# First swiglu of a two-layer encoder: modulation in four blocks of 256 channels, weight chunks begun two k at a time, six low parts on GpSimd

## Chip, cores and metric

The kernel runs on one core of one Trainium2 chip. The metric is the device time of one execution in microseconds (us); runs are compared by their median. Names of engines: PE is TensorE's matmul side, PEld its weight loads, DVE is VectorE, ACT is ScalarE, POOL is GpSimd, SP is SyncE, whose queue issues all DMAs of this kernel.

## What is computed

A two-layer encoder over 256 tokens of 1024 channels, all in float32. Each layer is swiglu, token mixer, swiglu; each of these sublayers is wrapped alike, with shift, scale and gate computed from a vector c by a 1024 x 9216 matrix per layer:

```python
sc = jax.nn.silu(c)
mod = (sc @ ada_w[i] + ada_b[i]).reshape(B, 9, D)

def modulated_sublayer(x, mod, g_pre, g_post, fn, weight):
    shift, scale, gate = mod[:, 0], mod[:, 1], mod[:, 2]
    h = rmsnorm(x, g_pre) * (1.0 + scale) + shift
    y = rmsnorm(fn(h), g_post)
    return x + weight * (1.0 + gate) * y

def swiglu(h, w_in, w_out):          # w_in 1024 x 5632, w_out 2816 x 1024
    gate, up = jnp.split(h @ w_in, 2, axis=-1)
    return (jax.nn.silu(gate) * up) @ w_out
```

So nothing of the first swiglu can be multiplied before the first 2048 columns of `ada_w[0]` (8 MB: shift and scale) have been loaded, summed and applied.

## The kernel before

The 256 tokens are two tiles t = 0, 1 of 128. A swiglu (class `FFN`) runs over 11 chunks c of 256 hidden channels. For a chunk and a token tile, `inn` multiplies h by 8 k-tiles of 128 channels (512 output columns: 256 gate, 256 up), `act` applies silu and the product, `tr` transposes, and `outt` multiplies by the output weights `wo` into an accumulator. `unit(c, t)` is one such step, with `tr` and `outt` of earlier steps after it.

**Two-part operands.** Most weights are multiplied as two float32r parts: ACT makes the high part (a cast, L263), DVE the low part (a subtraction, L271: raw minus high), and PE makes three passes per k (`mm3`, L98 to L100). Weights "in whole" are multiplied in float32 as loaded, with no work on ACT or DVE; PE then shows two records per k (L794).

**Bulk.** All weight loads are a queue of tasks (class `Bulk`): load, ACT work, DVE work. Loads go through four raw buffers of 1 MB (`N_RAW`), which are used in turn; a load into a buffer waits until the buffer's last reader is done, and SP issues in order, so what stands behind it waits too. Modulation vectors other than the first two come in four pieces of 1 MB (`ada_vector`), summed on DVE in two steps of 1024 columns each (L352: sum += weight row x sc[k]). `plan` spreads such pieces between the weights of a swiglu.

**The first swiglu.** Shift (m = 0) and scale (m = 1) come in halves of 512 channels, each of two 1 MB pieces (`ada_half`); a half takes 8 DVE steps of 512 columns per vector. PE sums over partitions (`finish_cols`, L361) and transposes the scaled x (L562); DVE or ACT modulates (L582, L576). `head_first` runs chunks 0 to 2 while the second half of the channels is on its way: chunks 0 and 2 multiply the first four k in float32, chunk 1 in two parts; `rest` does the other four k of all three, and then come `tr` and `outt` of chunks 0 and 1. Chunk 3 and later ones are `unit` steps. Four pieces of the next sublayer's modulation (`ss1[0]` to `ss1[3]`) stand between the weights of this stretch; the other 18 pieces of f0's plan are spread over chunks 3 to 9.

Of the kernel before, what the change touches and what calls it, by code (L numbers as in the profile page):

```python
# [39 lines left out]
def kernel(  # L40
# [127 lines left out]
    class Bulk:  # L168
        """A queue of loads, each followed by its work on ACT (high parts) and on DVE (low parts, sums).
        Loads run N_RAW entries ahead of the DVE work."""  # L170

# [36 lines left out]
        def high(self, key):  # L208
            """Emit the ACT work up to and including key (whose load must be out)."""
# [47 lines left out]
    def split_work(name, st, put, width=2048):  # L257
        """The two parts of a raw tile (st[0]); put() gets their tiles."""
# [8 lines left out]
        def low(lo_=0, hi_=width, engine=nc.vector):  # L267
# [48 lines left out]
    def ada_half(layer, m, hf, accs, pieces=(1, 1)):  # L316
        """Half of the channels of mod[layer, m], in two 1 MB pieces."""
        st = {}
        wv = ada_w[layer].rearrange("(p k) n -> p k n", k=KD)
        c0 = m * D + hf * 512  # L320

        def load(q):
            def go():
                raw = raw_tile(f"adah{m}{hf}{q}")
                rv = raw.rearrange("p (k n) -> p k n", k=4)
                for k in range(0, 4, 4 // pieces[q]):
                    ks = slice(k, k + 4 // pieces[q])
                    nc.sync.dma_start(rv[:, ks, :], wv[:, 4 * q + ks.start : 4 * q + ks.stop, c0 : c0 + 512])
                st[q] = raw

            return go

        def compute(q):
            def go():
                rv = st.pop(q).rearrange("p (k n) -> p k n", k=4)
                if m not in accs:
                    accs[m] = rowp.tile([P, D], F32, tag="acc", name=f"aacc{layer}{m}", bufs=3)
                acc = accs[m][:, hf * 512 : (hf + 1) * 512]
                for j in range(4):
                    ada_step(acc, rv[:, j, :], 4 * q + j)  # L340
                if q == 1:
                    bulk.fin.append(lambda: finish_cols(layer, m, range(hf * 4, hf * 4 + 4))(acc))

            return go

        return [(("adah", m, hf, q), load(q), None, compute(q)) for q in range(2)]
# [1328 lines left out]
```

## Time and profile before

| | |
|---|---|
| time, median of 3 runs (lowest to highest) | 929.82 us (928.57 to 932.09) |
| profiled execution, first to last instruction (span) | 928.2 us |
| PE busy | 902.1 us, 97% of the span |
| DVE, ACT, POOL busy | 705.8, 441.1, 41.9 us |
| moved by DMA | 235.28 MB, 253 GB/s over the span |
| mean granted TensorE clock | 0.992 of full |

The profiled execution's own time is given by its span alone; what lies around a span is seen in the 1.6 us between it and the median of the runs. An engine's busy time says little of what bounds the kernel where stages differ, so the rows are read by stage: the head (to 78 us, when chunk 3 begins), the body of the first swiglu (78 to 220 us), and the rest. "DMA share" is the mean busy share of the 16 DMA engines (it can read a little over 1), "PEclk" the granted clock as a share of 2.4 GHz. A releaser in brackets is what ended an engine's idle time.

### The profile page before, as it was taken

The numbers are of one execution on the slowest core, as the hardware profiler recorded it, in microseconds if no ns is written. First come the engines' busy times: TensorE is split into PE (matmuls) and PEld (weight loads), VectorE is DVE, ScalarE is ACT, GpSimd is POOL, SyncE is SP. The second block draws the span as 40 slices with busy tenths as digits, with TensorE's granted clock in tenths as the row PEclk, the third lists the DMA queues.
The fourth block names the chain that finished last, engine by engine and source line by source line (L and its number), as shares of the span: only waits on it lengthen the run. The fifth ranks groups of instructions, "written<-read, shape, count | busy, mean of one in ns | idle before, by whom it ended". The sixth has DMA issues, their size and how long they took to land.

```text
span 928.2 us, 11193 instructions
## 1 busy us (share of the span) xinstructions
PE 902.1 (97%) x4251; PEld 741.1 (80%) x4251; DVE 705.8 (76%) x856; ACT 441.1 (48%) x661; POOL 41.9 (5%) x56
## 2 busy tenths in 40 slices
PE   4999999999999999999999999999899999999997
PEld 3578887887888888888888888888798888888885
DVE  5898888788867998897867987766898765656553
ACT  2345443345645434334643534337699654343421
POOL 0000000000000000000000000001163000000000
PEclk9999999999999999999999999998999999999999
DMA  9989998996358998897469899960133558857601
GB/s 324 370 313 352 364 372 311 345 373 210 137 181 287 376 342 323 303 365 268 137 203 371 320 350 322 346 234 32 53 130 100 173 156 278 292 194 259 226 1 45
DMA packets 135973, 235.28 MB, mean 253 GB/s; under 512 B 5628, under 2 KB 98415, under 8 KB 135664
## 3 DMA queue, kind: packets, MB, share of 16 engines
q1 hardware_dynamic: 135920, 234.58, 72.6%
q8 instruction: 33, 0.54, 0.2%
q14 instruction: 20, 0.16, 0.0%
HBM read 233.51 MB, written 1.05 MB: 253 GB/s over the span
## 4 chain that ended last, share of the span: by engine, by line
PE 89%; DVE 4%; ACT 3%; issue 2%; DMA 1%; POOL 0%; SPq 0%; DVEq 0%; POOLq 0%; ACTq 0%
PE acc L747 25%; PE in L100 16%; PE in L98 16%; PE in L99 16%; PE accm L1314 2%; PE ps_g L724 2%; PE ps_h L562 1%; PE ps_mod L361 1%; DVE aacc L352 1%; PE in L794 1%; PE accp L965 1%; DMA adah<-in_ada_w_dram 1%; ACT p L1228 1%; DMA wi<-in_ffn_w_in_dram 1%; PE ps_turn L391 1%
## 5 line engine op out<-in xcount | busy, mean ns | idle before, releaser
L352 DVE SCALAR_TENSOR_TENSOR aacc<-ada,sc,aacc 128x1024 f32<-128x1024 f32 (+1 forms) x113 | 143.8, 1273 | 11.3 <-DMA ada<-in_ada_w_dram 9.1
L708 ACT ACTIVATE sil<-in 128x256 f32<-128x256 f32 x84 | 32.2, 383 | 247.7 <-PE in L100 240.4
L710 DVE TENSOR_TENSOR g<-in,sil 128x256 f32<-128x256 f32 x84 | 35.2, 420 | 52.4 <-ACT sil L708 52.3
L95 DVE TENSOR_TENSOR gL<-ps_g,gH 128x256 fp32r<-128x256 f32 x88 | 36.7, 417 | 23.6 <-ACT gH L94 23.5
L94 ACT CAST gH<-ps_g 128x256 fp32r<-128x256 f32 x88 | 32.4, 368 | 45.1 <-PE ps_g L724 45.0
L503 POOL TENSOR_TENSOR r<-ms,mhalf 128x1 f32<-128x1 f32 x24 | 13.6, 565 | 838.4 <-DVE ms L501 838.4
L724 PEld LDWEIGHTS ps_g<-ident,g 128*128 128x128 f32 x176 | 24.7, 140 | 11.5
L724 PE MATMUL ps_g<-ident,g 128*128 128x128 f32 x176 | 33.6, 272 | 0.0
L508 ACT ACTIVATE junk<-x 128x512 bf16<-128x512 f32 x24 | 15.1, 631 | 21.4 <-DVE x L535 11.3
L361 PE MATMUL ps_mod<-ones,aacc 128*128 128x1 f32 x96 | 12.7, 259 | 10.1 <-DVE cols L150 9.9
L576 ACT ACTIVATE hs<-ps_h,mod,mod 128x128 f32<-128x128 f32 x48 | 18.1, 458 | 8.4 <-DVE mod L377 5.0
L361 PEld LDWEIGHTS ps_mod<-ones,aacc 128*128 128x128 f32 x96 | 13.0, 210 | 11.2 <-DVE cols L150 10.1
L352 DVE SCALAR_TENSOR_TENSOR aacc<-adah,sc,aacc 128x512 f32<-128x512 f32 x28 | 21.0, 752 | 0.9
L582 DVE TENSOR_SCALAR hs<-ps_h,mod,mod 128x128 f32<-128x128 f32 x48 | 16.4, 404 | 5.2 <-PE ps_h L562 4.9
L535 DVE SCALAR_TENSOR_TENSOR x<-tmp,r,x 128x512 f32<-128x512 f32 x23 | 16.3, 749 | 2.2 <-POOL r L503 1.2
L1238 POOL TENSOR_SCALAR p<-p,rs 128x256 f32<-128x256 f32 x16 | 16.1, 1008 | 28.6 <-ACT p L1228 15.3
L554 ACT ACTIVATE xr<-x,r 128x512 f32<-128x512 f32 x12 | 8.7, 722 | 17.4 <-POOL r L503 17.4
L1228 ACT ACTIVATE p<-s,nm 128x256 f32<-128x256 f32 x32 | 14.9, 471 | 3.1 <-DVE nm L1220 2.6
L593 DVE TENSOR_TENSOR hTL<-hs,hTH 128x512 fp32r<-128x512 f32 x24 | 15.6, 688 | 0.4
L562 PE MATMUL ps_h<-ident,xr 128*128 128x128 f32 x96 | 14.3, 292 | 0.5 <-ACT xr L554 0.3
L271 DVE TENSOR_TENSOR wo10L<-wo,wo10H 128x2048 fp32r<-128x2048 f32 x4 | 9.2, 2293 | 7.4 <-ACT wo10H L263 7.4
L1263 PE MATMUL att<-pT,v 128*128 128x256 f32 x52 | 13.8, 389 | 0.5 <-ACT pT L1255 0.3
(498 smaller groups left out, 2892.7 us busy)
## 6 DMA issues: line engine op xcount, KB each, us to landing
wi<-in_ffn_w_in_dram SPq DMA_DIRECT2D x176, 512.0 KB, 5.9
ada<-in_ada_w_dram SPq DMA_DIRECT2D x64, 1024.0 KB, 6.4
wo<-in_ffn_w_out_dram SPq DMA_DIRECT2D x44, 1024.0 KB, 6.2
adah<-in_ada_w_dram SPq DMA_DIRECT2D x6, 1024.0 KB, 10.3
mwo<-in_mla_w_o_dram SPq DMA_DIRECT2D x4, 1024.0 KB, 5.4
bc<-in_ada_b_dram SPq DMA_DIRECT2D x12, 256.0 KB, 6.7
bc<-in_norm_g_dram SPq DMA_DIRECT2D x12, 256.0 KB, 7.4
adah<-in_ada_w_dram SPq DMA_DIRECT2D x4, 512.0 KB, 11.9
```

The lines of the kernel that those rows point to most:

```text
L94: nc.scalar.copy(h, src)
L95: nc.vector.tensor_sub(lo, src, h.bitcast(F32))
L98: nc.tensor.matmul(ps, lhsT=lh, rhs=rh, start=first, stop=False)
L99: nc.tensor.matmul(ps, lhsT=lh, rhs=rl, start=False, stop=False)
L100: nc.tensor.matmul(ps, lhsT=ll, rhs=rh, start=False, stop=last)
L352: nc.vector.scalar_tensor_tensor(acc, w, sc[:, k : k + 1], acc, op0=ALU.mult, op1=ALU.add)
L361: nc.tensor.matmul(ps[:, j : j + 1], lhsT=acc[:, (j - j0) * P : (j - j0 + 1) * P], rhs=ones[:, 0:1], start=True, stop=True,)
L708: nc.scalar.activation(sil, ps[:, 0:CW], AF.Silu)
L710: nc.vector.tensor_mul(g, ps[:, CW : 2 * CW], sil)
L724: nc.tensor.transpose(ps[:, a * P : (a + 1) * P], g[:, a * P : (a + 1) * P], ident)
L747: nc.tensor.matmul(acc[hf], lhsT=lhs[:, a, :], rhs=rhs[:, a, hf * 512 : (hf + 1) * 512], start=f, stop=l)
L1228: nc.scalar.activation(p[:, t * S : (t + 1) * S], ps[:, t * S : (t + 1) * S], AF.Exp, bias=nm[:, t : t + 1], accum_out=sm[:, t : t + 1],)
```

## The change

- Shift and scale of the first swiglu come in four blocks of 256 channels, one raw tile of 1 MB per vector and block (`ada_block`), in two DMAs (four for the first scale block). A block takes 8 DVE steps of 256 columns per vector.
- `head_first` is written anew. Per block b of 256 channels (2 k-tiles): sums, reduction, modulation, then those two k of chunks 0, 1 and 2 for both token tiles. Chunk 0 is multiplied in float32 for all k, chunk 1 for the first four k, chunk 2 always in two parts. Weights of these chunks are loaded two k at a time (`load_whole`, `load_raw`), chunk 2's first two blocks into one raw tile `wrc2`, later blocks of chunks 1 and 2 into `wrb2` and `wrb3`.
- DVE makes the low parts of these weights, but for chunk 2's in blocks 2 and 3, which POOL makes. The output weights' low parts of chunks 3 to 8 are made by POOL too (`low_out`).
- The modulation pieces `ss1[0]` to `ss1[3]` move from the head to f0's plan: 22 pieces instead of 18 over chunks 3 to 9. `Bulk.limit` holds the queue back until the head's own loads are out.
- Small ones: the loads of `norm_g` and `ada_b` rows are issued behind the first block and x0; the columns made of them are copied by ACT instead of DVE; in the head `pre_scale` lets DVE scale the half that is needed first; 5 and 4 warming matmuls instead of 6 and 4.

The core of the diff:

```diff
+    def ada_block(m, b, acc, pieces):
+        st = []
+        wv = ada_w[0].rearrange("(p k) n -> p k n", k=KD)
+        c0 = m * D + b * BW
+        def load():
+            rv = raw_tile(f"adab{m}{b}").rearrange("p (k n) -> p k n", k=KD)
+            n = KD // pieces
+            for k in range(0, KD, n):
+                nc.sync.dma_start(rv[:, k : k + n, :], wv[:, k : k + n, c0 : c0 + BW])
+            st.append(rv)
+        def steps(ks=range(KD)):
+            for k in ks:
+                ada_step(acc[:, b * BW : (b + 1) * BW], st[0][:, k, :], k)
+        return load, steps
...
+            def loads(b):
+                if b < 2:
+                    load_whole(0, b)
+                    load_whole(1, b)
+                    load_raw(2, b, "c2", b)
+                else:
+                    load_whole(0, b)
+                    load_raw(1, b, f"b{b}", 0)
+                    load_raw(2, b, f"b{b}", 1)
+            def split_block(b, low2=nc.vector):
+                for t in range(NT):
+                    split_h(t, b)
+                for c in (1, 2):
+                    if (c, b) in parts:
+                        part_high(c, b)
+                        part_low(c, b, nc.vector if c == 1 else low2)
+            def sum_up(b, mid=nop):
+                bank = tr_tile(f"ps_modb{b}")
+                ada[0, b][1]()
+                mid()
+                reduce(0, b, bank)
+                ada[1, b][1]()
+                reduce(1, b, bank)
+                add()
...
+            sum_up(1)
+            for t in range(NT):
+                modulate(t, 1, True)
+                multiply(0, t, 1)
+            split_block(1)
+            ada[1, 2][0]()
+            loads(2)
+            ada[0, 3][0]()
+            turn_next(2)
+            for c in (1, 2):
+                for t in range(NT):
+                    multiply(c, t, 1)
+            sum_up(2, lambda: ada[1, 3][0]())
+            for t in range(NT):
+                modulate(t, 2, True)
+                multiply(0, t, 2)
+            loads(3)
+            split_block(2, nc.gpsimd)
+            more_bulk(1)
...
-        def low(lo_=0, hi_=width, engine=nc.vector):
+        def low(lo_=0, hi_=width, engine=low_engine or nc.vector):
...
-    f0, f2, f3, f5 = FFN(0, 0), FFN(0, 1), FFN(1, 0), FFN(1, 1)
+    f0 = FFN(0, 0, {c: nc.gpsimd for c in range(3, 9)})
+    f2, f3, f5 = FFN(0, 1), FFN(1, 0), FFN(1, 1)
...
-    f0.plan(ss1[4:] + gate(0, 0, in_parts=False) + ss2[:4] + gate(0, 1, hold="pool") + ss2[4:6], first_chunk=4, extra_out=2)
+    f0.plan(ss1 + gate(0, 0, in_parts=False) + ss2[:4] + gate(0, 1, hold="pool") + ss2[4:6], first_chunk=4, extra_out=2)
```

**DVE in the head.** In these rows `aacc00` and `aacc01` are the sums of shift and scale, `mod` their columns, `hs` the modulated h, `hTL` its low part. Before, from the first half's modulation to the sums of the second half:

```order
L582 TENSOR_SCALAR hs00_212<-ps_h00_176,mod01_209,mod00_139 128x128 x4
L350 TENSOR_SCALAR aacc00_111<-adah010_119,sc_93 128x512
L352 SCALAR_TENSOR_TENSOR aacc00_111<-adah010_119,sc_93,aacc00_111 128x512 x3
L593 TENSOR_TENSOR hTL0_173<-hs00_212,hTH0_172 128x512
L588 CAST hTH1_174<-hs10_217 128x512
L593 TENSOR_TENSOR hTL1_175<-hs10_217,hTH1_174 128x512
L271 TENSOR_TENSOR wi10L_245<-wi10_125,wi10H_243 128x2048
L352 SCALAR_TENSOR_TENSOR aacc00_111<-adah011_157,sc_93,aacc00_111 128x512 x4
```

Changed, from block 0's modulation to block 1's columns; what follows for blocks 2 and 3 has the same form:

```order
L834 TENSOR_SCALAR hs00_202<-ps_h0_171,mod01_198,mod00_156 128x128 x2
L492 SCALAR_TENSOR_TENSOR ms_208<-s2_178 128x1
L547 TENSOR_SCALAR xr1_212<-x1_81,r_210 128x512
L95 TENSOR_TENSOR hTL0_99<-hs00_202,hTH0_98 128x256
L95 TENSOR_TENSOR hTL1_101<-hs10_217,hTH1_100 128x256
L798 TENSOR_TENSOR wi20L_234<-wrc2_122,wi20H_233 128x1024
L341 TENSOR_SCALAR aacc00_96<-adab01_125,sc_93 128x256
L343 SCALAR_TENSOR_TENSOR aacc00_96<-adab01_125,sc_93,aacc00_96 128x256 x7
L341 TENSOR_SCALAR aacc01_97<-adab11_157,sc_93 128x256
L343 SCALAR_TENSOR_TENSOR aacc01_97<-adab11_157,sc_93,aacc01_97 128x256 x7
L365 TENSOR_TENSOR mod00_156<-ps_modb1_256,cols_95 128x2
L365 TENSOR_TENSOR mod01_198<-ps_modb1_256,cols_95 128x2
```

The sums of the next channels stood ahead of `hTL` and the weight's low part; now they stand behind them.

**SP's queue in the head**, changed, with the semaphores that each DMA waits for (`DVE` is a wait for the last DVE reader of the raw buffer):

```order
L619 DMA wrc2_122<-in_ffn_w_in_dram 128x2x256 [waits DMAHW2_49]
L330 DMA adab02_193<-in_ada_w_dram 128x4x256 [waits DMAHW3_49,DVE_49]
L330 DMA adab02_193<-in_ada_w_dram 128x4x256 [waits DMAHW4_49]
L330 DMA adab12_294<-in_ada_w_dram 128x4x256 [waits DMAHW5_49,DVE_49]
L330 DMA adab12_294<-in_ada_w_dram 128x4x256 [waits DMAHW6_49]
L619 DMA wi01_297<-in_ffn_w_in_dram 128x2x256 [waits DMAHW7_49]
```

The raw tiles are taken in the order adab00, adab10, wrc2, adab01, adab11, adab02, adab12, so that `adab12` goes into `wrc2`'s buffer, whose last reader is the DVE subtraction of block 1 (the second `wi20L`, behind block 1's sums).

**POOL**, changed; the eight subtractions in the middle are new there:

```order
L494 TENSOR_TENSOR r<-ms,mhalf 128x1 x2
L798 TENSOR_TENSOR wi21L<-wrb_300,wi21H 128x1024
L798 TENSOR_TENSOR wi21L<-wrb_368,wi21H 128x1024
L273 TENSOR_TENSOR wo3L<-wo_658,wo3H 128x2048
L273 TENSOR_TENSOR wo4L<-wo_787,wo4H 128x2048
L273 TENSOR_TENSOR wo5L<-wo_926,wo5H 128x2048
L273 TENSOR_TENSOR wo6L<-wo_1070,wo6H 128x2048
L273 TENSOR_TENSOR wo7L<-wo_1213,wo7H 128x2048
L273 TENSOR_TENSOR wo8L<-wo_1347,wo8H 128x2048
L494 TENSOR_TENSOR r<-ms,mhalf 128x1 x16
```

Before, POOL held only the small powers (`r`) up to the attention; these subtractions were on DVE.

## Rows read from the trace of the kernel before

**Rows 1.** The page: busy time of each engine.
```profile
PE 902.1 (97%) x4251; PEld 741.1 (80%) x4251; DVE 705.8 (76%) x856; ACT 441.1 (48%) x661; POOL 41.9 (5%) x56
```

**Rows 2.** Busy time by stage: PE, PEld, DVE, ACT, POOL, PEclk, DMA share, GB/s.
```profile
24.20:78.01 53.81, 53.11 (x211) 37.19 (x211) 47.97 (x59) 24.07 (x30) 0.00 (x0) 0.97 0.98 343
78.01:220.00 141.99, 141.99 (x649) 116.22 (x648) 118.98 (x116) 58.10 (x66) 1.10 (x2) 1.00 0.99 352
...
48.00:52.00 4.00, 3.96 (x17) 2.77 (x16) 3.96 (x3) 1.96 (x2) 0.00 (x0) 1.00 0.22 59
```

**Rows 3.** Waits of PE from 60 to 300 us: total, times, longest.
```profile
PE in L98 <- DVE hTH L588: 0.5, 1, 0.5
```

**Rows 4.** Timeline of the head: start, us, instruction, idle before and releaser.
```profile
2.11 0.94 SPq L328 DMA_DIRECT2D adah<-in_ada_w_dram  x2
...
7.60 0.48 DVE L350 TENSOR_SCALAR aacc<-adah,sc 128x512 f32<-128x512 f32 x1 [6.22 <-DMA adah<-in_ada_w_dram]
...
11.51 0.63 ACT L508 ACTIVATE junk<-x 128x512 bf16<-128x512 f32 x1 [8.91 <-DMA x<-in_x_dram]
...
27.00 1.90 ACT L263 CAST wi10H<-wi 128x2048 fp32r<-128x2048 f32 x1 [1.19 <-DMA wi<-in_ffn_w_in_dram]
```

**Rows 5.** The chain that ended last, 22 to 43 us: start, us, what.
```profile
22.25 1.07 PE ps_mod L361 x8
...
23.74 0.42 DVE hs L582
...
24.20 8.83 PE in L794 x16
...
33.26 0.23 PE first L99
...
39.80 3.43 PE first L794 x8
```

**Rows 6.** Durations: timeline (start first) and groups by shape (busy, mean ns).
```profile
8.12 5.48 DVE L352 SCALAR_TENSOR_TENSOR aacc<-adah,sc,aacc 128x512 f32<-128x512 f32 x7
...
44.51 1.51 ACT L576 ACTIVATE hs<-ps_h,mod,mod 128x128 f32<-128x128 f32 x4 [0.59 <-DVE mod L377]
...
47.66 1.91 ACT L263 CAST wi11H<-wi 128x2048 fp32r<-128x2048 f32 x1 [0.67 <-DMA wi<-in_ffn_w_in_dram]
...
L352 DVE SCALAR_TENSOR_TENSOR aacc<-ada,sc,aacc 128x1024 f32<-128x1024 f32 x111 | 142.3, 1282 | 11.3 <-DMA ada<-in_ada_w_dram 9.1
...
L271 DVE TENSOR_TENSOR wo0L<-wo,wo0H 128x1024 fp32r<-128x1024 f32 x6 | 7.3, 1217 | 0.0
...
L503 POOL TENSOR_TENSOR r<-ms,mhalf 128x1 f32<-128x1 f32 x24 | 13.6, 565 | 838.4 <-DVE ms L501 838.4
...
L94 ACT CAST gH<-ps_g 128x256 fp32r<-128x256 f32 x88 | 32.4, 368 | 45.1 <-PE ps_g L724 45.0
```

**Rows 7.** An output step in the chain; PE's first matmul of chunk 3.
```profile
69.75 2.73 PE acc L747 x12
...
78.01 0.39 PE L98 MATMUL in<-wi30H,hTH 128*128 128x512 f32 x1
```

**Rows 8.** POOL and DVE in the attention, timelines of the two engines.
```profile
679.92 1.29 POOL L271 TENSOR_TENSOR mwo0L<-mwo,mwo0H 128x512 fp32r<-128x512 f32 x1
...
685.80 1.30 POOL L271 TENSOR_TENSOR mwo0L<-mwo,mwo0H 128x512 fp32r<-128x512 f32 x1
...
680.70 0.78 DVE L1203 TENSOR_TENSOR ql<-qm,qh 128x256 fp32r<-128x256 f32 x1
...
684.15 0.43 DVE L1203 TENSOR_TENSOR ql<-qm,qh 128x256 fp32r<-128x256 f32 x1
...
686.79 0.59 DVE L1203 TENSOR_TENSOR ql<-qm,qh 128x256 fp32r<-128x256 f32 x1
```

**Rows 9.** Chunk 10's weights: the low part on DVE, their first matmul on PE.
```profile
188.12 2.29 DVE L271 TENSOR_TENSOR wi100L<-wi,wi100H 128x2048 fp32r<-128x2048 f32 x1 [1.72 <-ACT wi100H L263]
...
191.25 0.39 PE L98 MATMUL in<-wi100H,hTH 128*128 128x512 f32 x1
```

More of the change, by code (lines that the diff above doesn't have):

```diff
@@ L172, in __init__ @@
         def __init__(self):
+            self.limit = 0
             self.tasks = []
@@ L188, in advance @@
                 out = sum(t[3] is not None for t in self.tasks[self.done : self.loaded])
-                if out >= N_RAW:
+                if out >= self.limit:
                     break
@@ L255, with split_work @@
     bulk = Bulk()
-    def split_work(name, st, put, width=2048):
+    def split_work(name, st, put, width=2048, low_engine=None):
         def high(lo_=0, hi_=width):
@@ L314, in ada_vector @@
         return [(("ada", layer, m, q), load(q), None, compute(q)) for q in range(4)]
[L316 to L346, printed above, removed]
+    BW = 2 * P
+    def ada_block(m, b, acc, pieces):
[12 more added lines that the diff above has]
+        return load, steps
     def ada_step(acc, w, k):
@@ L550, in pre_xr, with pre_scale @@
         return pre_scale(t, rstd(s2, 1.0))
-    def pre_scale(t, r):
+    def pre_scale(t, r, act_half=0):
         xr = rowp.tile([P, D], F32, tag="xr", name=f"xr{t}")
-        nc.scalar.activation(xr[:, 0:512], xt[t][:, 0:512], AF.Copy, scale=r)
-        nc.vector.tensor_scalar(xr[:, 512:1024], xt[t][:, 512:1024], r, None, op0=ALU.mult)
+        a, v = (slice(hf * 512, (hf + 1) * 512) for hf in (act_half, 1 - act_half))
+        nc.scalar.activation(xr[:, a], xt[t][:, a], AF.Copy, scale=r)
+        nc.vector.tensor_scalar(xr[:, v], xt[t][:, v], r, None, op0=ALU.mult)
         return xr
@@ L661, in put @@
                 self.wo[c] = (h.rearrange("p (a d) -> p a d", a=2), lo.rearrange("p (a d) -> p a d", a=2))
-            return (("wo", self.layer, self.fi, c), load, *split_work(f"wo{c}", st, put))
+            return (("wo", self.layer, self.fi, c), load, *split_work(f"wo{c}", st, put, low_engine=self.low_out.get(c)))
         def plan(self, ada, first_chunk=0, extra_out=None, last=NCH - 1):
@@ L782, in head @@
             return hT1
-        def head_first(self, hT, h0, halves):
-            pss = {}
-            for c in range(3):
-                if c > 0:
-                    a = acc_tile(c - 1, f"first{c}")
-                for t in range(NT):
-                    pss[c, t] = psum.tile([P, 512], F32, tag="in", name=f"in0{t}") if c == 0 else a[t]
-                    for k in range(4) if c != 1 else ():
-                        nc.tensor.matmul(
-                            pss[c, t], lhsT=h0[t][:, k * P : (k + 1) * P], rhs=self.wi[c, 0][:, k, :],
-                            start=k == 0, stop=False,
-                        )
-                    if c == 1:
-                        self.mm_in(pss[c, t], c, t, hT[t], range(4))
-                    next(halves)
-            def rest(c, t):
-                if c == 0:
-                    hh, hl = hT[t]
-                    wh, wl = self.wi[0, 1]
-                    for lh, w in ((hh, wh), (hl, wh), (hh, wl)):
-                        for k in range(4, KD):
-                            nc.tensor.matmul(
-                                pss[c, t], lhsT=lh[:, k, :], rhs=w[:, k % 4, :], start=False,
-                                stop=lh is hh and w is wl and k == KD - 1,
-                            )
-                else:
-                    self.mm_in(pss[c, t], c, t, hT[t], range(4, KD))
-            self.need_in(0, 1)
-            rest(0, 0)
-            self.need_in(1, 1)
@@ L832, in head_first @@
+            self.act(pss[2, 1], 2, 1)
             self.need_out(1)
@@ L834, in head_first @@
             self.tr(1, 1)
-            rest(2, 1)
-            self.act(pss[2, 1], 2, 1)
             self.need_in(3, 0)
@@ L1386, in ffn_tail @@
         )
-    bulk.until(("adah", 0, 0, 1))
-    turn_g()
-    turn_b()
-    bulk.finish_pe()
-    s20 = first_rstd(0)
-    xr0 = pre_xr(0, s20)
-    bulk.until(("adah", 1, 0, 0))
-    bulk.finish()
-    s21 = first_rstd(1)
-    xr1 = pre_xr(1, s21)
-    hT = [new_hT(0), new_hT(1)]
-    turned = [turn_half(0, 0, xr0)]
-    warm(6, "acc11", 1)
-    turned += [turn_half(1, 0, xr1, psum.tile([P, 512], F32, tag="acc10", name="ps_h10", bufs=1))]
-    warm(4, "acc11", 1)
-    bulk.until(("adah", 1, 0, 1))
-    bulk.finish()
-    parts = [mod_half(t, 0, ps, hT[t], 0, 0, t == 1) for t, ps in enumerate(turned)]
-    def first_halves():
-        bulk.until(("adah", 0, 1, 0))
-        yield
-        for high, low, _ in parts:
-            high()
-            low()
-        bulk.until(("wi", 0, 0, 1, 0))
-        yield
-        bulk.until(("adah", 0, 1, 1))
-        bulk.finish()
-        late = [turn_half(0, 1, xr0)]
-        yield
-        yield
-        bulk.until(("adah", 1, 1, 1))
-        f0.high_in(0, 1)
-        bulk.finish()
-        late += [turn_half(1, 1, xr1)]
-        late = [mod_half(t, 1, ps, hT[t], 0, 0, t == 0) for t, ps in enumerate(late)]
-        for high, _, _ in late:
-            high()
-        for _, low, _ in late:
-            low()
-        yield
-        yield
-    f0.head_first(hT, [p[2] for p in parts], first_halves())
+    hT = f0.head_first()
     turn_late = load_columns_late()
```

173 lines of the change are left out of this document (143 added, 30 removed).

## Prediction

> **What bounds the kernel now.** The page's busy times come first: PE works 902 of 928 us [rows 1], so no more than 26 us are idle on PE in the whole program, and time can be won only where PE has not begun or waits. The table by stage comes next [rows 2]. From 24.2 to 78.0 us (chunk 3 begins at 78.01, [rows 7]) PE is busy 53.1 of 53.8 us, and from there to 220 us all the time. The longest of its three waits from 60 to 300 us is 0.5 us [rows 3]. So the program ends later or earlier by as much as chunk 3 begins later or earlier, if the body stays without waits. The same table shows that the body's cover is thin. The DMA engines are 98 and 99% busy in the two stages, with one gap of note (22% from 48 to 52 us, about 3 us lost). DVE is busy 119 of 142 us in the body, so 23 us are left over there. Chunk 10's first low part is ready at 188.12 + 2.29 = 190.41 and its first matmul starts at 191.25 [rows 9]: at the body's end the weights are 0.8 us ahead.
>
> **Where PE begins.** Before, PE starts at 24.20 [rows 5], after 4 MB of modulation weights. The queue's pace: x0, 2.5 MB into it, is there at 11.5 us, wi10, 5.5 MB later, at 27.0 [rows 4]: 2.8 us per MB. Now the first load is issued 0.9 us earlier (two small loads moved behind it; 2.11 before). So x0 (1.5 MB in) lands at 11.5 - 2.8 - 0.9 = 7.8 and the first scale block (2.6 MB in) at 10.8.
>
> A DVE step of 512 columns takes 5.48 / 7 = 0.78 us, one of 1024 columns 1.28 [rows 6]. So 256 columns are worth 0.26, and a 256 step takes 0.52. The first step of a block, a plain product (0.48 at 512, [rows 4]), is put at 0.36. A vector's block is then 0.36 + 7 x 0.52 = 4.0 us, and both vectors take 8.0. The four blocks take 32 us, where the halves took 28 x 0.78 + 4 x 0.48 = 24: the smaller step is dearer by its fixed part.
>
> The first shift block is in from 5 to 6.5 us and summed by 9.0. DVE then asks for x0's squares, which ACT has at 10.9 (rows landed and copied by 9.3, two squares 1.5). The scale block with the scaling of x0 in its middle (0.5) is done at 15.7. Reduction and columns took 23.74 - 22.25 = 1.5 with eight records [rows 5]; with four I take 1.1. Block 0's columns are ready at 16.8, and PE begins at 17.2, **7 us earlier**.
>
> **From block to block.** Here DVE's order decides. After the columns of a block, ACT modulates both tiles (four of 1.51 / 4 us: 1.5), casts h twice (0.37 each) and makes a high part of 1024 columns (half of 1.91: 0.95) [rows 6]. Only then comes DVE's low part (1.2), and behind it the next sums (8.0) and columns (1.1). With 0.2 for hand-overs that is **13.7 us per block**. PE's work per block is less: a float32 k takes 2 x 0.43 = 0.86 us (8 records in 3.43), a two-part k 3 x 0.23 = 0.69 [rows 5]. That is 8 x 0.86 + 4 x 0.69 in block 1, with 1.5 for reductions and transposes 11 us. So PE waits some 3 us in every block. Block 0 is longer, because token tile 1's factor (POOL 0.57, [rows 6]), scaling and transposes lie in between: 6.4 to the low part's end, then 8.0 + 1.1, so 15.5. The columns come at 16.8, 32.3, 46.0 and 59.7 us.
>
> **POOL in the head.** Block 2 also has POOL's subtraction of 1024 columns. The trace shows it for 512 only, 1.29 us [rows 8]: twice that, 2.6, is the upper bound, and with POOL's smallest operation (0.57) as the fixed part 2.0 the lower. I take 2.4. Beside it DVE's own subtraction of 256 columns, all in SBUF, took 0.78 and 0.59 instead of 0.43 in the two cases in which POOL's was running as it began; both end some 0.27 us after POOL's [rows 8]. So DVE stood still while POOL worked, and I add 2.4 to block 3: 62.1 us. The other bound is 0, if POOL gets in between others at no cost.
>
> The page "SBUF — State Buffer" of the Trainium skill (SBUF: two separate sides) has this as a rule: a DVE instruction with two SBUF inputs and a GpSimd one that reads SBUF lock each other out for a whole instruction. By that rule the 2.4 stands; without it the sum is 2.4 less. The trace agrees where it can be seen.
>
> **To chunk 3.** After block 3's columns PE still has 4 float32 k and 8 two-part k (8.9), four output steps of 2.73 (10.9, [rows 7]), five small transposes (1.5) and 0.5 to begin; it waits 0.6 for chunk 1's low part and 1.2 for wo1's, which DVE makes last. That is 23.6, and chunk 3 begins at 62.1 + 23.6 = 85.7 instead of 78.0: **7.7 us later**. Within the 54 us of the head, 7 are won at its start, and the waits of four blocks and the dearer passes (8 k in float32 instead of two parts: 8 x 0.17 = 1.4) cost twice that.
>
> **The DMA queue says the same.** `adab12` waits for block 1's low part, at 32.3 + 4.4 = 36.7; what stands before it (9.1 MB) has landed by 7.8 + 7.6 x 2.8 = 29. A first byte needs some 2 us after its issue (2.11 to 7.60 for a first MB worth 2.8, [rows 4], leaves 2.7). So the engines stand still for about 9 us, where before they lost 3. Shorter gaps follow at wi31, which waits for POOL's second subtraction. The body's extra modulation pieces only make up for what the head did not load. Against 0.8 us of lead at the end [rows 9], 9 - 3 - 0.9, and 2 to 4 for the later gaps, is 7 to 9 us late. I count it once, since both delays pass together.
>
> **The body.** 4 more pieces cost DVE 8 x 1.28 = 10.2 us; six low parts of 2.29 leave it, 13.7. On POOL one takes between 3.5 (fixed part 0.57) and 4 x 1.29 = 5.2. Their holds are hidden in DVE's 23 free us as long as all six stay below 23 + 13.7 - 10.2 = 26.5, or 4.4 each. I take them as hidden. Warming matmuls, ACT's copies of the columns and the swapped halves of x cost nothing: PE or DVE waits for data beside them; uncovered, all are under 1 us.
>
> The profiled span would be 928.2 + 7.7 = 935.9; the median of the runs lies 1.6 above the span, so **937.5 us**.
>
> **Rivals.** *The sums keep up (faster).* If PE never waits after 17.2, its work to chunk 3 is 24 x 0.86 + 24 x 0.69 + 10.9 + 1.5 + 5.0 for reductions and transposes, 54.6 us: chunk 3 at 71.8, or 73.8 if the first 16 records run at a lower clock again (8.83 for 16 against 3.43 for 8, [rows 5]). That is 4.2 to 6.2 us less, 924 to 926. It needs a block on DVE to take under 11 us, which rows 6 do not give. 10%.
>
> *A small step is cheaper.* With a 256 step at half of a 512 step (0.39) and no hold by POOL, a block takes 11.5, the columns come at 15.7, 29.0, 40.5 and 52.0, and chunk 3 at 75.6: 2.4 less, eaten in part by the DMA gap (still 6 us). 927 to 931, no change. 23%.
>
> *POOL holds DVE in the body (still slower).* If a low part of 2048 columns holds DVE for 5.2 us, six need 31, 5 more than the 26.5 free, and chunks 8 to 10 wait: 942 to 944, and up to 948 if their loads are late as well. It decides from 4.4 us per hold. The Trainium skill's "GPSIMD Engine Reference" (Elementwise — side-by-side cycle accounting) gives 4497 ns for such a float32 operation of 2048 columns; by that figure the holds are 27 us, and this rival is worth 0.5 us. No row here shows that width. 22%.
>
> **The numbers.** The forecast has 45%. A change of under 0.5%, 4.6 us, cannot be told from none by a measurement of this kernel. Slower by more is nearly all of the forecast and the last rival: 63%. Faster by more is half of the first rival and the edge of the second: 7%. The rest, 30%, is no change. The range from 926 to 948 leaves out the best half of the first rival, the worst of the last, and what I have not thought of. The forecast's own range is 933 to 942.
>
> **What would show it.** PE's first matmul at 17 us; steps of 256 columns at 0.52; columns every 13 to 14 us with PE idle before each block; some 9 us without DMA around 30 to 39; chunk 3 at 83 to 86; DVE steps that end with POOL's subtractions. I am wrong if block 3's columns come before 52 us, or if the body makes up or loses more than 2 us.

## The result and the profile after

The changed kernel takes 955.9 us (median of 4 runs, 953.51 to 959.1) against 929.2 in the same rounds: the ratio is 1.028, 95% interval 1.026 to 1.031. It is slower, as forecast, but by 27 us where I had 7.7, and it lies outside my range. The profiled execution has a span of 957.3, 29.1 more than before; it is the slowest of the four runs, 3.2 us above their median.

The page of the changed kernel: busy times, and of the 40 slices PE, POOL, PE's clock and DMA.

```profile
PE 913.2 (95%) x4241; PEld 743.2 (78%) x4241; DVE 716.8 (75%) x881; ACT 442.4 (46%) x678; POOL 74.4 (8%) x64
...
PE   5888999979999999999999999999999999999997
...
POOL 0020131110000000000000000000055000000000
PEclk9979999998989999999999999999999999999999
DMA  9956999989535999989458998973122556867601
```

PE is now idle for 44 us instead of 26 [rows 1]. The third and fourth slice (48 to 96 us) have the DMA engines at 5 and 6 tenths. Where the time went, by PE's matmuls with the first weights of chunk 3 and of chunk 10, and by the pooling's first ones (`z`), changed kernel (the first number behind the durations is the first start):

```profile
L98 PE MATMUL in<-wi30H,hTH x8: 389/389/389, 91.5 to 102.0; 128*128 128x512 f32 x8
L98 PE MATMUL in<-wi100H,hTH x8: 389/552/793, 215.3 to 241.8; 128*128 128x512 f32 x8
L98 PE MATMUL z<-pwH,hTH x16: 278/283/415, 251.8 to 267.7; 128*128 128x256 f32 x16
```

Before, these stood at 78.0, 191.3 [rows 7, 9] and 223.1. So chunk 3 begins 13.5 later, chunk 10 24.0, pooling 28.7, and behind pooling hardly anything is added. All of it is lost in the first swiglu: half before chunk 3, half behind it.

**The head.** DVE in the changed kernel, from block 1's columns to block 3's sums (timeline; in brackets the idle time before an instruction and what ended it):

```profile
33.93 0.16 DVE L368 SCALAR_TENSOR_TENSOR mod<-mod,cols 128x2 f32<-128x2 f32 x1
36.02 0.76 DVE L95 TENSOR_TENSOR hTL<-hs,hTH 128x256 fp32r<-128x256 f32 x2 [1.93 <-ACT hTH L94]
37.27 1.22 DVE L798 TENSOR_TENSOR wi20L<-wrc,wi20H 128x1024 fp32r<-128x1024 f32 x1 [0.49 <-ACT wi20H L793]
38.41 0.35 DVE L341 TENSOR_SCALAR aacc<-adab,sc 128x256 f32<-128x256 f32 x1
38.80 3.61 DVE L343 SCALAR_TENSOR_TENSOR aacc<-adab,sc,aacc 128x256 f32<-128x256 f32 x7
...
47.55 0.22 DVE L365 TENSOR_TENSOR mod<-ps_modb,cols 128x2 f32<-128x2 f32 x2 [1.24 <-PE ps_modb L352]
...
51.15 1.23 DVE L798 TENSOR_TENSOR wi11L<-wrb,wi11H 128x1024 fp32r<-128x1024 f32 x1 [0.49 <-ACT wi11H L793]
52.29 2.45 DVE L341 TENSOR_SCALAR aacc<-adab,sc 128x256 f32<-128x256 f32 x1
54.78 3.61 DVE L343 SCALAR_TENSOR_TENSOR aacc<-adab,sc,aacc 128x256 f32<-128x256 f32 x7
```

This is the chain of the forecast: high parts on ACT, low parts on DVE, sums, columns. The columns of the four blocks are ready at 16.8, 34.1, 48.0 and 63.8; I had 16.8, 32.3, 46.0 and 62.1.

**DVE held by GpSimd.** GpSimd's first subtraction in the head, and the first two of the six in the body; then DVE beside these two (the same timelines):

```profile
52.14 2.45 POOL L798 TENSOR_TENSOR wi21L<-wrb,wi21H 128x1024 fp32r<-128x1024 f32 x1 [33.87 <-ACT wi21H L793]
...
101.01 4.61 POOL L273 TENSOR_TENSOR wo3L<-wo,wo3H 128x2048 fp32r<-128x2048 f32 x1 [30.59 <-ACT wo3H L265]
119.56 4.61 POOL L273 TENSOR_TENSOR wo4L<-wo,wo4H 128x2048 fp32r<-128x2048 f32 x1 [13.94 <-ACT wo4H L265]
...
101.94 6.07 DVE L343 SCALAR_TENSOR_TENSOR aacc<-ada,sc,aacc 128x1024 f32<-128x1024 f32 x2 [1.91 <-DMA ada<-in_ada_w_dram]
...
108.60 2.60 DVE L343 SCALAR_TENSOR_TENSOR aacc<-ada,sc,aacc 128x1024 f32<-128x1024 f32 x2
...
120.47 4.24 DVE L341 TENSOR_SCALAR aacc<-ada,sc 128x1024 f32<-128x1024 f32 x1 [1.69 <-DMA ada<-in_ada_w_dram]
```

Two steps that take 2.60 alone take 6.07, and a product of 0.75 takes 4.24. They end 2.39 and 0.54 us after GpSimd's instruction, each 0.2 less than its own time: DVE stood still until GpSimd was done. All six together hold DVE for 21.5 us, 3.2 to 3.9 each. GpSimd's rows last 4.59 to 4.61.

**The DMA engines.** By stretches (us from the start): PE, PEld, DVE, ACT, POOL busy, PE's clock, DMA share, GB/s; and the packets of the first 90 us. The kernel before, then the changed one:

```profile
0.00:50.00 50.00, 35.05 (x134) 24.00 (x134) 35.57 (x63) 15.68 (x25) 1.79 (x8) 0.97 0.96 338
50.00:90.00 40.00, 39.56 (x179) 31.84 (x179) 36.39 (x34) 21.22 (x22) 0.00 (x0) 1.00 0.98 345
90.00:170.00 80.00, 80.00 (x365) 65.18 (x364) 70.45 (x67) 32.63 (x33) 0.00 (x0) 1.00 0.98 351
...
DMA packets 18356, 30.68 MB, mean 341 GB/s; under 512 B 852, under 2 KB 11446, under 8 KB 18352
```

```profile
0.00:50.00 50.00, 34.38 (x114) 21.89 (x115) 29.54 (x73) 13.42 (x32) 1.83 (x8) 0.95 0.97 307
50.00:90.00 40.00, 33.73 (x127) 23.23 (x126) 26.00 (x40) 18.57 (x27) 4.89 (x2) 0.89 0.57 186
90.00:170.00 80.00, 78.80 (x363) 64.39 (x362) 70.89 (x56) 30.13 (x31) 18.42 (x4) 1.00 0.95 337
170.00:220.00 50.00, 40.12 (x168) 31.04 (x168) 40.26 (x32) 16.27 (x17) 9.18 (x2) 0.93 0.90 312
...
DMA packets 20273, 22.81 MB, mean 253 GB/s; under 512 B 1034, under 2 KB 19245, under 8 KB 20269
```

From 50 to 90 the engines are 57% busy: 40 x 0.43 = 17 us of standing still. By 90 us 7.87 MB fewer have come in. The body of the kernel before moves 351 GB/s with its engines 98% busy, so little can be caught up there: 7.87 / 0.351 = 22.4 us of arrears (what the engines have not yet moved, in us at the body's rate). Some 1.5 MB of this, 4.4 us, are missing at 50 us already, though the engines were as busy as before (0.97 and 0.96): they moved 307 GB/s instead of 338. The new loads come in rows of 256 columns, and 19245 packets instead of 11446 are under 2 KB; that their size is the reason was not tested. And while GpSimd works the share falls once more, to 95 and 90%. The chain of work that ended last shows why (changed kernel, start, us, what):

```profile
95.21 6.64 DMA ada<-in_ada_w_dram
...
101.94 4.76 DVE aacc L343
...
111.11 2.30 DVE wi50L L273
...
113.43 7.02 DMA ada<-in_ada_w_dram
...
120.47 4.25 DVE aacc L341
```

A load, the held sums, what stands behind them on DVE up to `wi50`'s low part, which frees a buffer, the next load, and the next held sum: in this loop a hold passes on to the next load.

### The profile page after: what moved, and what is told of

Same layout as the page of the kernel before. It is cut to its first block, busy times and chain, and to the rows that moved or that the text cites. A ratio compares the mean times of both kernels' runs of the same rounds, so it can differ in the third digit from the quotient of the medians.

```text
span 957.3 us, 11269 instructions
## 1 busy us (share of the span) xinstructions
PE 913.2 (95%) x4241; PEld 743.2 (78%) x4241; DVE 716.8 (75%) x881; ACT 442.4 (46%) x678; POOL 74.4 (8%) x64
## 4 chain that ended last, share of the span: by engine, by line
PE 74%; DVE 12%; DMA 6%; ACT 4%; issue 3%; SPq 0%; POOL 0%; DVEq 0%; POOLq 0%; ACTq 0%
PE acc L730 20%; PE in L100 13%; PE in L99 13%; PE in L98 13%; DVE aacc L343 5%; DMA ada<-in_ada_w_dram 4%; PE accm L1464 2%; DMA wi<-in_ffn_w_in_dram 2%; PE ps_g L707 2%; PE in L850 2%; PE ps_h L554 1%; DVE aacc L341 1%; PE accp L1115 1%; PE ps_mod L352 1%; PE warm L108 1%
## 5 line engine op out<-in xcount | busy, mean ns | idle before, releaser
L343 DVE SCALAR_TENSOR_TENSOR aacc<-ada,sc,aacc 128x1024 f32<-128x1024 f32 (+1 forms) x113 | 158.6, 1404 | 17.9 <-DMA ada<-in_ada_w_dram 15.7
L95 DVE TENSOR_TENSOR gL<-ps_g,gH 128x256 fp32r<-128x256 f32 x88 | 36.7, 417 | 24.2 <-ACT gH L94 24.1
L707 PEld LDWEIGHTS ps_g<-ident,g 128*128 128x128 f32 x176 | 24.4, 140 | 15.1 <-DVE gL L95 2.1
L343 DVE SCALAR_TENSOR_TENSOR aacc<-adab,sc,aacc 128x256 f32<-128x256 f32 x56 | 27.1, 485 | 2.0
L850 PE MATMUL in<-wi,hs 128*128 128x512 f32 x32 | 22.6, 864 | 4.7 <-ACT hs L832 3.7
L832 ACT ACTIVATE hs<-ps_h,mod,mod 128x128 f32<-128x128 f32 x14 | 5.3, 458 | 35.5 <-DVE mod L368 33.0
L499 ACT ACTIVATE junk<-x 128x512 bf16<-128x512 f32 x24 | 15.2, 632 | 12.7 <-DVE x L526 11.3
L850 PEld LDWEIGHTS in<-wi,hs 128*128 128x128 f32 x32 | 8.3, 274 | 14.9 <-issue 6.2
L98 PE MATMUL in<-wi100H,hTH 128*128 128x512 f32 x32 | 14.1, 439 | 6.0 <-ACT wi100H L265 6.0
L574 DVE TENSOR_SCALAR hs<-ps_h,mod,mod 128x128 f32<-128x128 f32 x40 | 13.7, 404 | 5.9 <-PE ps_h L554 5.7
L568 ACT ACTIVATE hs<-ps_h,mod,mod 128x128 f32<-128x128 f32 x40 | 15.1, 457 | 4.6 <-PE ps_h L554 4.5
L341 DVE TENSOR_SCALAR aacc<-ada,sc 128x1024 f32<-128x1024 f32 x16 | 15.5, 966 | 1.7 <-DMA ada<-in_ada_w_dram 1.7
L99 PE MATMUL in<-wi100L,hTH 128*128 128x512 f32 x32 | 13.6, 425 | 1.5 <-DVE wi100L L273 1.5
```

The costliest lines, as they stand in the source:

```text
L95: nc.vector.tensor_sub(lo, src, h.bitcast(F32))
L98: nc.tensor.matmul(ps, lhsT=lh, rhs=rh, start=first, stop=False)
L99: nc.tensor.matmul(ps, lhsT=lh, rhs=rl, start=False, stop=False)
L341: nc.vector.tensor_scalar(acc, w, sc[:, 0:1], None, op0=ALU.mult)
L343: nc.vector.scalar_tensor_tensor(acc, w, sc[:, k : k + 1], acc, op0=ALU.mult, op1=ALU.add)
L707: nc.tensor.transpose(ps[:, a * P : (a + 1) * P], g[:, a * P : (a + 1) * P], ident)
```

## The experiments

Two theories. **Queue**: the head leaves the DMA engines behind, and the first swiglu ends later by what they have not moved. **Holds**: GpSimd's six low parts cost the body its 15 us. For the head the question was what sets 14 to 17 us per block. All kernels ran with the kernel before beside them; ratios are to that. Pooling's start is from each profiled execution, against 223.1 before.

### Low parts back on DVE, and the holds alone

```diff
-    f0 = FFN(0, 0, {c: nc.gpsimd for c in range(3, 9)})
+    f0 = FFN(0, 0)
```

> The changed kernel with the six output weights' low parts back on DVE (GpSimd keeps its two subtractions in the head). Holds theory (GpSimd's six holds of DVE, 21.5 us, are what the body loses): the body's 15 us come back but for the 13.7 us of DVE work that returns, which fits into DVE's free time: 941 to 945. Queue theory (at 91 us the DMA engines are already some 17 us behind, since they stood half idle from 50 to 90, and the body runs at their pace): at most the 8 us that they stand idle in the body (5% of 157) come back: 948 to 953.

948.33 us, ratio 1.019 (1.017 to 1.021). Pooling begins at 240.1. That is 7.6 us of the 27 (11.7 at pooling, in the profiled executions), near the most that the queue theory allows and far from the holds theory. The stretches:

```profile
90.00:170.00 80.00, 80.00 (x370) 65.96 (x370) 70.92 (x64) 31.12 (x33) 0.00 (x0) 1.00 1.00 359
170.00:220.00 50.00, 47.14 (x201) 37.47 (x200) 41.70 (x40) 16.28 (x17) 0.00 (x0) 0.97 0.96 352
```

The DMA share goes from 0.95 and 0.90 to 1.00 and 0.96: 4 + 3 = 7 us of engine time, nearly the whole gain. PE still waits for chunk 10.

The opposite: the kernel before, with only these six on GpSimd.

```diff
-        f0, f2, f3, f5 = FFN(0, 0), FFN(0, 1), FFN(1, 0), FFN(1, 1)
+        f0 = FFN(0, 0, {c: nc.gpsimd for c in range(3, 9)})
```

> The kernel before with only the six output weights' low parts (chunks 3 to 8) moved to GpSimd. Holds theory: DVE is held for six times some 3.6 us and no longer makes 13.7 us of low parts; the raw buffers come free later all the same, and the body loses 8 to 15 us: 937 to 944. Queue theory: the DMA queue has 0.8 us of lead in this kernel and each hold delays at most one or two buffers by 2 to 4 us: 929 to 935. Theory of the forecast (hidden in DVE's 23 free us): 928 to 930.

936.47 us, but spread from 927.54 to 941.14; ratio 1.005 (1.002 to 1.009). In the profiled execution pooling is 6.3 late, all of it at one place, where PE waits 3.4 us and then runs at a lower clock for some 6 us (0.53 granted from 150 to 154):

```profile
140.83 6.78 DVE L352 SCALAR_TENSOR_TENSOR aacc<-ada,sc,aacc 128x1024 f32<-128x1024 f32 x2
147.53 0.41 DVE L711 TENSOR_TENSOR g<-in,sil 128x256 f32<-128x256 f32 x1
...
PE ps_g L725 <- DVE g L711: 3.4, 1, 3.4
```

The gate `g` that PE transposes stands on DVE behind the held sums. In the kernel before it starts at 139.15, here at 147.53. Half of these 8.4 us are this hold, the other half was there when it began, behind the hold before. So a hold costs at the place where it falls, by what queues behind it, while 23 us of DVE's time are free elsewhere.

### The four extra pieces

```diff
-    f0.plan(ss1 + gate
+    f0.plan([ss1[i] for i in (0, 3, 4, 7)] + gate
```

> The changed kernel without the two middle quarters of each of the second sublayer's shift and scale (4 MB neither loaded nor summed: half of these two vectors is left out). Queue theory: the body is bound by the DMA engines, and 4 MB are 11 us of them: 943 to 946. Holds theory: 10.2 us less DVE work beside the holds: 946 to 951. If neither the queue nor DVE binds the body: 955.

948.41 us, 1.019 (1.017 to 1.021); in the profiled executions pooling begins 11.3 earlier (240.5), as much as 4 MB are worth, though the medians differ by 7.5 only.

The same pieces loaded, with their sums left out:

> The same four pieces loaded, but not summed (half of the second sublayer's shift and scale is left out): the DMA bytes stay, 10.2 us of DVE work go. Queue theory: little, 951 to 956, since the bytes still have to pass. Holds theory, in which DVE is what is short: as much as without the loads, 945 to 950.

952.67 us, 1.025 (1.021 to 1.029), pooling at 245.5. In the profiled executions the sums alone give 6.3 of the 11.3; by the medians they give 3.2 of 7.5, which the intervals can't tell from nothing. So neither theory has it alone, and which counts for more is not shown.

### The head

GpSimd's two subtractions in the head back on DVE (`split_block(2)` and `split_block(3)` without `nc.gpsimd`):

> The changed kernel with the two subtractions of blocks 2 and 3 (1024 columns each) back on DVE; the six in the body stay on GpSimd. If GpSimd's 2.45 us in block 2 costs block 3 the 2.1 us by which it held DVE, and the buffers of wo0 and wi31, which wait for these two subtractions, come 1.3 us earlier: 952 to 954. If DVE's own 1.23 us in their place cost the same again: 955 to 957, no change.

957.9 us, 1.028 (1.025 to 1.030): no change. Block 3's columns follow block 2's by 14.5 us instead of 15.8, so the hold did cost the block 1.3 more than DVE's own subtraction; but chunk 3 begins at 91.5 in both, and the gain is lost behind the columns.

The next block's first sums ahead of the low parts:

```diff
+            ada[0, 2][1]()
             split_block(1)
...
             def sum_up(b, mid=nop):
                 bank = tr_tile(f"ps_modb{b}")
-                ada[0, b][1]()
```

> The changed kernel with the shift's sums of the next block (4 us on DVE) put ahead of a block's low parts, so that DVE no longer waits 1.9 to 3.9 us for ACT's high parts in each block. DVE theory (DVE's order sets 13.7 to 15.8 us per block): blocks of 11.5 to 12.5, columns at 17, 29, 41 and 55, chunk 3 some 7 to 9 us earlier, the raw buffers too: 945 to 949. PE theory (PE's own 12 us per block at the low clock are as long): 2 to 4 us, 952 to 954.

953.06 us, 1.024 (1.021 to 1.027); chunk 3 at 87.6 instead of 91.5. That is half of what DVE's theory gave, and the time is in the range of the PE theory. DVE now stands ready and waits 4.82, 2.12 and 2.48 us for PE's reductions, which PE has queued behind all matmuls of the block (`ps_modb`, then the wait for ACT; PE's timeline of this kernel):

```profile
45.89 0.95 PE L352 MATMUL ps_modb<-ones,aacc 128*128 128x1 f32 x8
47.90 5.40 PE L850 MATMUL in<-wi,hs 128*128 128x512 f32 x8 [1.06 <-ACT hs L832]
```

Small matmuls in these waits:

```diff
                 reduce(0, b, bank)
+                fill(bank, 4)
                 ada[1, b][1]()
                 reduce(1, b, bank)
+                fill(bank, 6)
```

> The changed kernel with ten small matmuls per block in PE's waits (4 between the two reductions, 6 behind the second, blocks 1 to 3). PE theory (after each wait the eight float32 matmuls take 5.4, 5.4 and 6.0 us, where they took 3.4 at the full clock): they take 3.4 to 3.6, PE is ready ahead of DVE in blocks 1 and 2, and 0.5 + 0.9 + 2.6 us come back: 951 to 953. DVE theory: only block 3's 2.6 us count, 953 to 954. If the small matmuls stand in the way of the second reduction, nothing: 956.

963.73 us, 1.035 (1.032 to 1.038): 8 us worse. The clock did rise in blocks 1 and 2: their float32 passes take 3.70 us instead of 5.40; block 3's takes 6.30, no less than before. But I let the small matmuls write into the bank of the sums, so DVE's columns waited for the last of them, and each block grew by 0.9 to 1.4 us. Since DVE's chain sets the length of a block here, PE's shorter passes gave nothing back. Chunk 3 begins at 95.4.

All three together (no GpSimd, sums ahead, small matmuls):

> No subtraction on GpSimd, the sums ahead, and the small matmuls together: what the change costs without these three. If they add up (7.6 measured for the six in the body, 7 to 9 for the order, 3 for the clock, 1 for the head): 935 to 938. If the DMA queue's arrears remain (it stood still for 17 us from 50 to 90): 941 to 945. Below 929 only if the whole of the change's arrears came from these.

950.42 us, 1.020 (1.016 to 1.023). The small matmuls spoil it; without them:

> The same without the early reductions: no subtraction on GpSimd and the sums ahead. By the sum of what was measured apart (7.6 for the six subtractions, 4 for the order): 943 to 945. Chain theory: 6 to 12 us above the kernel with the early reductions. DMA theory: within 3 us of it.

939.22 us, 1.014 (1.008 to 1.019). Then, with that kernel, PE's reductions of the next block between its last two groups of matmuls (shown for block 2's sums, the others alike):

```diff
-            for c in (1, 2):
-                for t in range(NT):
-                    multiply(c, t, 1)
+            for t in range(NT):
+                multiply(1, t, 1)
+            multiply(2, 0, 1)
             sum_up(2, lambda: ada[1, 3][0]())
+            multiply(2, 1, 1)
```

> No subtraction on GpSimd, the sums ahead, and PE's reductions of the next block put between its last two groups of this block's matmuls instead of behind them. Chain theory (with the sums ahead, a block is PE's work plus the chain reduction, columns, ACT, in which PE idles 2 us and then runs the next float32 pass at half clock): DVE and PE overlap, blocks of 11.5 to 12.5, columns at 17, 29, 41 and 52, chunk 3 at 76 to 80 (91.5 in the changed kernel), DMA idle from 50 to 90 cut to 10 us or less: 930 to 938. DMA theory (the arrears of 17 us come from the number of raw buffers and not from the columns): chunk 3 earlier, but the body gives it back: 942 to 948.

940.27 us, 1.011 (1.007 to 1.014). The blocks' columns follow each other by 13.4, 11.0 and 11.9 us, and PE's passes run at the full clock:

```profile
30.86 3.60 PE L850 MATMUL in<-wi,hs 128*128 128x512 f32 x8
...
39.56 0.95 PE L352 MATMUL ps_modb<-ones,aacc 128*128 128x1 f32 x8
41.84 3.59 PE L850 MATMUL in<-wi,hs 128*128 128x512 f32 x8
```

Chunk 3 begins at 80.3, 11 us earlier than in the changed kernel and 3.6 earlier than without the early reductions, and yet the time is that of the kernel without them. The body gives it back: pooling is 10.4 late, with 4.09 MB, 11.7 us, not yet moved by 90. That is the queue's kind of end, though not its size: chunk 3 and the arrears both came down by some 3.6 us, and pooling by 0.8.

### The buffers

From 56 to 80 the DMA engines still stood idle for some 10.5 us in that kernel, each time until the low part of `wo0`, `wo1`, `wi30` or `wi31` freed its buffer. These come at once now, instead of behind the gates:

```diff
+            self.high_out(0)
             for t in range(NT):
                 modulate(t, 3, True)
                 multiply(0, t, 3)
+            self.need_out(0)
...
             self.act(pss[1, 0], 1, 0)
+            self.need_out(1)
             multiply(1, 1, 3)
...
+            self.need_in(3, 0)
             multiply(2, 1, 3)
...
-            self.need_in(3, 0)
+            self.need_in(3, 1)
             self.outt(1, 0)
...
```

> The kernel with the early reductions, and the low parts of wo0, wo1, wi30 and wi31 each made as soon as DVE has a gap, instead of behind the gates of block 3: the four raw buffers come free some 3 to 9 us earlier. Queue theory (what is left over at the end, +10 in the sublayer, is the 10.6 us for which the DMA engines stand still from 56 to 80, since the buffers wait for these low parts): 4 to 6 us of that stillness go, 933 to 936. If the arrears come from elsewhere in the body: 938 to 941.

935.14 us, 1.006 (1.004 to 1.008). Share and megabytes of this kernel:

```profile
50.00:90.00 40.00, 38.60 (x170) 29.76 (x169) 32.84 (x40) 22.75 (x29) 0.00 (x0) 1.00 0.88 304
...
DMA packets 22757, 28.36 MB, mean 315 GB/s; under 512 B 1147, under 2 KB 20704, under 8 KB 22752
```

The same earlier order in the changed kernel, without the other edits:

> The changed kernel with that earlier order of the four low parts alone. Queue theory: the DMA engines stand still 17 us from 50 to 90; 4 to 6 of these go: 949 to 952. If GpSimd's holds and DVE are what bounds the body: 955 to 957.

952.56 us, 1.026 (1.023 to 1.030). Its profiled execution has pooling 7 us earlier than the changed kernel's, the medians 3.3 us; by the intervals it can't be told from the changed kernel.

Last, two tests of both terms on the kernel with the earlier buffers: the six low parts put back on GpSimd, and the 4 MB taken out.

> The kernel with the earlier buffers, its six output weights' low parts put back on GpSimd. If arrears and holds add up: pooling begins 6.6 + 6 = 12.6 us later than in the kernel before, the run is 6 to 8 us above the kernel with the earlier buffers, 941 to 943. If the holds cost only where the weights are already late (here they are 2 us behind at most): 0 to 3 us, 935 to 938.

945.85 us, 1.016 (1.015 to 1.018): 10.7 more. Holds and arrears add up, and more than I expected.

> The kernel with the earlier buffers, without the two middle quarters of each of the second sublayer's shift and scale (4 MB neither loaded nor summed: half of these vectors is left out). If the 5 us that are left are DMA arrears, 4 MB (11.4 us) more than cover them, and pooling begins with what chunk 3 is late, 0.6 us, or before: 928 to 931. If they are something else in the body: 934 to 936.

931.81 us, 1.001 (1.000 to 1.003). Pooling begins at 222.9, 0.2 before the kernel before. So the 5 us that were left come from the four pieces: from their 4 MB, as the queue theory has it, or from their 10.2 us of sums, which went with them; no run on this kernel separates the two.

The two terms over the kernels that load all (chunk 3's and pooling's delay against before, the arrears as MB missing at 90 us divided by 0.351, all in us, from one profiled execution each; the changed kernel's is 3 us above its median):

| kernel | chunk 3 | arrears | pooling | pooling less arrears |
|---|---|---|---|---|
| changed | 13.5 | 22.4 | 28.7 | +6.3 |
| head's two on DVE | 13.5 | 21.3 | 27.7 | +6.4 |
| sums ahead | 9.6 | 19.6 | 24.4 | +4.8 |
| small matmuls | 17.4 | 26.1 | 33.0 | +6.9 |
| buffers earlier only | 9.9 | 17.1 | 21.6 | +4.5 |
| four pieces unsummed | 12.2 | 21.3 | 22.4 | +1.1 |
| before, six on GpSimd | 0.0 | 0.0 | 6.3 | +6.3 |
| buffers earlier, six on GpSimd | -0.5 | 6.2 | 15.4 | +9.2 |
| changed, six on DVE | 12.1 | 21.3 | 17.0 | -4.3 |
| all three | 15.4 | 22.5 | 21.2 | -1.3 |
| sums ahead, no GpSimd | 5.9 | 15.4 | 11.2 | -4.2 |
| reductions early | 2.3 | 11.7 | 10.4 | -1.3 |
| buffers earlier | 0.6 | 6.6 | 6.5 | -0.1 |

With the six on GpSimd pooling is later than the arrears by 4.5 to 9.2 (by 1.1 where four pieces' sums are left out), without them earlier by 0.1 to 4.3. So something is caught up after all: with the six on DVE the changed kernel moves 359 GB/s from 90 to 170 against 351, which is 1.8 us. The pairs that differ in the six alone differ by 10.6 and 9.3 in this column and 6.3 on the kernel before; in the medians by 7.6, 10.7 and 6.2.

The table alone does not separate the arrears from chunk 3's own delay: without the six, pooling is later than chunk 3 by 4.9 to 8.1 in every row. What speaks for the arrears is the pair with and without early reductions (chunk 3 3.6 earlier, pooling 0.8) and the kernel with the earlier buffers (chunk 3 0.6 late, pooling 6.5). And counted up to 220 us instead of 90, with the 4 MB taken off where they are not loaded, the missing megabytes give pooling's delay in all fifteen kernels to within 2.4 us (in the changed one 76.25 - 65.39 = 10.86 MB, 30.9 us, against 28.7), those with the six on GpSimd included. So the holds, too, go with transfers that come late; but a count at the end does not say which was late first, the transfer or the work that frees its buffer.

No version tried is faster than the kernel before. The best two that compute all, the one with the earlier buffers and the kernel before with six on GpSimd, are 0.5% slower.

## Why the prediction was wrong

**Where PE begins** held: the first matmul at 17.30 (forecast 17.2). PE's timeline of the changed kernel, and its busy times from 64 to 68 us (PE's clock is the last number but two):

```profile
17.30 3.78 PE L850 MATMUL in<-wi,hs 128*128 128x512 f32 x4 [0.96 <-DVE hs L834]
...
64.42 6.03 PE L850 MATMUL in<-wi,hs 128*128 128x512 f32 x8 [1.06 <-ACT hs L832]
...
83.44 0.73 PE L730 MATMUL acc<-wo1L,gH 128*128 128x512 f32 x2 [2.32 <-DVE wo1L L273]
...
64.00:68.00 4.00, 3.58 (x5) 1.51 (x6) 1.76 (x3) 3.91 (x8) 0.01 (x1) 0.50 0.72 248
```

**From block to block** held to 2.0 us, nearly all of it in block 0 (17.3 instead of 15.5), and a step of 256 columns took 3.61 / 7 = 0.52, as put. GpSimd's 1024 columns took 2.45 (taken: 2.4) and held DVE for 2.1.

**To chunk 3** was 27.7 us instead of 23.6. 2.6 of the 4.1 are the clock: block 3's float32 pass took 6.03 instead of 3.43 behind a wait, with 0.50 granted from 64 to 68 (1.2 of 2.4 GHz). I had allowed for that in a rival and not here. 1.1 more is the wait for `wo1`'s low part, 2.32 instead of 1.2. So the head came out at 13.5 instead of 7.7, of which 1.7 is the columns and 4.1 this.

**The DMA queue says the same** is the step that failed. I put the arrears at 7 to 9 us and counted them once with the head's delay. Counting once was right in kind, as far as the runs show: without the six on GpSimd pooling is late by the arrears or up to 4.3 less, and chunk 3's own delay does not come on top. But the arrears are 22.4. I looked for the gap at 30 to 39, where `adab12` should wait for `wrc2`'s buffer until 36.7. It didn't: it got another buffer than the order of the raw tiles had made me think. SP's queue of the changed kernel has the last of three `adab` loads out at 23.30 + 6.71 = 30.01, right after the sums of `adab01` freed a buffer:

```profile
23.30 6.71 SPq L330 DMA_DIRECT2D adab<-in_ada_w_dram  x3
30.05 1.02 SPq L619 DMA_DIRECT2D wi<-in_ffn_w_in_dram  x2
```

The load that did wait for block 1's low part came out at 38.52, and the share from 30 to 40 was 0.87. The gaps came from 50 to 90, which I had written off as "shorter" and as 2 to 4 us. SP's queue there, and DVE's low part of `wo0`:

```profile
54.62 4.17 SPq L640 DMA_DIRECT2D wo<-in_ffn_w_out_dram  x2
62.32 9.05 SPq L619 DMA_DIRECT2D wi<-in_ffn_w_in_dram  x4
76.89 0.37 SPq L640 DMA_DIRECT2D wo<-in_ffn_w_out_dram  x1
83.42 3.45 SPq L619 DMA_DIRECT2D wi<-in_ffn_w_in_dram  x4
...
74.58 2.29 DVE L273 TENSOR_TENSOR wo0L<-wo,wo0H 128x2048 fp32r<-128x2048 f32 x1 [1.32 <-ACT wo0H L265]
```

Each load goes out just when the last reader of a buffer is done: GpSimd's low part in block 2 (54.59), block 3's sums (58.39 and 62.30), GpSimd's low part in block 3 (70.43), and then the low parts of `wo0` (76.87) and `wo1` (83.39), which DVE makes in the order of the gates. The rest of the arrears, 4.4 us at 50 us, came with busy engines that moved less, a term that I did not have. I had followed the queue to the fourth block and stopped where the four buffers hold the weights of the next stage.

**The body** failed too: "I take them as hidden". GpSimd's instruction takes 4.60 against my threshold of 4.4; by that reckoning six cost 27.6 - 26.5 = 1.1 us, and by the holds themselves, 21.5 in all, nothing. They cost 6 to 11. The mechanism of the rival, that GpSimd's holds of DVE make the body late, was right, the threshold wrong: it compared the sum of the holds with the sum of DVE's free time. But DVE's free time lay where nothing waited, and five of the six holds fell on the sums that free the DMA's buffers, which had next to no slack (98% busy before), and the low parts or the gate that PE needs stand behind these sums.

The Trainium skill's page "SBUF — State Buffer" (SBUF: two separate sides) says that whichever of the two engines starts first keeps a shared pair of ports for its whole instruction. The trace agrees: 4.24 us for a product of 0.75. The Trainium skill's "GPSIMD Engine Reference" (Elementwise — side-by-side cycle accounting) gives 4497 ns for 2048 columns; the rows here have 4.59 to 4.61.

What stays open: why the six cost nothing in some executions of the kernel before (927.54) and 10 us in others, since only one was profiled; and how the loss that is left divides between the four pieces' bytes and their sums.

## What to carry to other kernels

Where a stage is bound by DMA, ask of every change what it does to the release of the buffers, and count the megabytes that have come in by the stage's start: divided by the stage's rate, the missing ones gave the delay to within some 4 us here where nothing else held the buffers, and an earlier compute start by itself won little (0.8 of 3.6 us). Follow the queue past the part that was rewritten, until the buffers turn over at the stage's rate again. Free time of an engine covers added work only if it lies where the work falls; a sum of holds against a sum of idle time does not say it.

## What was not expected of the hardware

The hold also falls on DVE's product with a column of constants, which reads one tensor: 2.45 instead of 0.35 us at 256 columns, 4.24 instead of 0.75 at 1024. And GpSimd gives way in turn: in the kernel before with six on GpSimd one of its subtractions lasted 5.16 where the others lasted 4.60.
